# Each PSUM bank of the recurrence and of attention first takes a product of constants

## The chip, the cores and the metric

The kernel runs as one program on one core of a Trainium2 chip. The metric is the time of one launch on the device in microseconds, lower is better. The engines are TensorE (PE in the profile, with its weight loads as PEld), VectorE (DVE), ScalarE (ACT), GpSimd (POOL) and SyncE (SP, which issues most of the transfers). Each engine works through its own list of instructions in order.

## The reference: one inference step of a hybrid decoder layer

512 prompt tokens with 16 learned meta tokens ahead of them, and 8 samples of 4 tokens each, go through one layer with the same weights. All data is float32.

```
h    = rmsnorm(x);  proj = h @ w_in          # 1024 -> 2560 columns: 1792 for the recurrence, 768 for attention
y_rw = rwkv7_time_mix(proj[:, :1792])        # 8 heads x 64; per token S = S*w + (S a) b' + v k',  y = S r
y_at = window_attention(proj[:, 1792:])      # 8 query heads, 2 key heads, the last 128 positions, sinks
x    = x + concat(y_rw, y_at) @ w_out
x    = x + peer(rmsnorm(x))                  # 8 heads choose 16 of 16384 experts each by product keys:
                                             # sum over 128 chosen k of gelu(h . eu[k]) * gate[k] * ev[k]
y    = rmsnorm(x)
```

The outputs are y of prompt and samples, the key and value windows, the state of the recurrence and the last normalised row.

## The kernel before, in words

The prompt is cut into four tiles of 128 tokens, 0 to 3; meta tokens and samples are short pieces of their own. The work falls into a front part (to about 1110 us in the profile) and a dense part.

**Front part.** `project` (L218 and around) multiplies the normalised input by w_in, block of 128 columns by block; the second half of the tokens (`project_rest`, 314 columns a product, PSUM tag pD) stands beside the first pieces of the recurrence. For each tile `rwkv_prep` (L333 to L390, banks pA and pQ) forms the factors of the recurrence, and `wkv_local` (banks pB; pC for the meta tokens) solves a triangular system of 128 steps in blocks: for each of five levels, and for two groups of four heads, a transposition by the identity (L182 on XT), four products of 64 columns into one bank (L492), a copy out by ACT, four products of 64 columns into the next bank (L497), and a masked copy by DVE. `wkv_chain` carries the state across tiles. `attend_prompt`, `attend_sample`, `sample_wkv` and what is around them use banks of the tag pC. `rest` multiplies by w_out (L918) and w_query (L952) into banks of the tag pD, with weights that DMA brings, and picks experts on DVE.

Of the tags pB and pC there are two banks of [128, 512] float32 each. A call of `pB()` or `pC()` hands out the next of the two: whoever writes it first waits until the readers of its last contents are done. 434 banks are handed out in this way in the front part.

**Gathers.** For prompt tile 0, then for the samples and for tile 3, rows of expert tables are fetched one chosen expert at a time (L1032, an indirect DMA that POOL issues, 512 KB into one of five buffers `gat`); DVE forms the dot product or adds the row (L126). They are put in beside the front part, from `first_gathers` on.

**Dense part.** For tiles 1 and 2 all 16384 experts are multiplied (L1401 to L1480).

**What sets the order.** The program is written stage by stage, and a scheduler orders each engine's list by a simulated clock of its own: an instruction is put in when, in that simulation, its inputs and its bank are there. So more work on one engine shifts the order on others. Gathers carry a mark that keeps them behind the front's own work.

Of the kernel before, what the change touches and what calls it, by code (L numbers as in the profile page):

```python
# [46 lines left out]
BF16 = mybir.dt.bfloat16  # L47
# [66 lines left out]
def hymba_step(ctx, tc, x_prompt, x_sample, cache_k, cache_v, state_wkv, state_shift, meta, norm1_g, w_in, mu, w0,  # L114
# [3 lines left out]
    A, G, T, DM = nc.scalar, nc.gpsimd, nc.tensor, nc.sync  # L118
# [14 lines left out]
    def _t(pool, tag, bufs, shape, dt=F32):  # L133
        uid[0] += 1
        return pool.tile(list(shape), dt, tag=tag, name=f"{tag}_{uid[0]}", bufs=bufs)
# [29 lines left out]
    ident = p0.tile([128, 128], F32, name="ident")  # L165
    DM.dma_start(ident, const[:, _OFF["ident"][0]:_OFF["ident"][0] + 128])
    cst = cp.tile([128, _MSO], F32, name="cst")
# [86 lines left out]
    def pA():  # L254
        return _t(pe, "pA", 1, [128, 512])

    def pB():
        return _t(pp, "pB", 2, [128, 512])

    def pC():  # L260
        return _t(pp, "pC", 2, [128, 512])

    def pD():
        return _t(pp, "pD", 2, [128, 512])
# [342 lines left out]
    def wkv_chain(r, l, ycat):  # L607

        ends = r["ends"]
        S0 = st("S0", 1, [128, 4, 64])  # L610
        V.tensor_tensor(S0, Sst, bc(ends[:, :, 1:2], [128, 4, 64]), OP.mult)
        for hb in range(2):
            pb = 64 * hb
            A.copy(Sbd[pb:pb + 64, :, hb, :], S0[pb:pb + 64])
        pC_ = pC()[:, 0:256].rearrange("p (a b) -> p a b", a=4)
        for blk in range(4):
            T.matmul(pC_[:, blk, :], l["M"][:, blk, :], S0[:, blk, :], start=True, stop=True)
        V.tensor_tensor(Sst, pC_, l["Sl"], OP.add)
        V.tensor_tensor(Sst, Sst, bc(ends[:, :, 0:1], [128, 4, 64]), OP.mult)
        pY = pC()  # L620
        for blk in range(4):
            T.matmul(pY[:, 128 * blk:128 * blk + 128], l["R2T"][:, blk, :], Sbd[:, blk].rearrange("p a b -> p (a b)"),
                     start=True, stop=True)
        Y = st("gn", 2, [128, 512])
        V.tensor_tensor(Y, pY, l["Yl"].rearrange("p a b -> p (a b)"), OP.add)
        gn_out(r, Y, ycat)

    def meta_state(r):
        n = r["n"]
        pm = pC()  # L630
        for blk in range(4):
            for hb in range(2):
                h = 2 * blk + hb
                hc = slice(64 * h, 64 * h + 64)
                o = pm[64 * hb:64 * hb + 64, 64 * blk:64 * blk + 64]
                T.matmul(o, r["Bn"][:n, hc], r["RW"][:n, 0, h, :], start=True, stop=False)
                T.matmul(o, r["Kn"][:n, hc], r["Vn"][:n, hc], start=False, stop=True)
        V.tensor_tensor(Sst, pm[:, 0:256].rearrange("p (a b) -> p a b", a=4), bc(r["ends"][:, :, 0:1], [128, 4, 64]),
                        OP.mult)
# [521 lines left out]
    with ExitStack() as px:  # L1161
# [36 lines left out]
        def transposed(h, half, rows):  # L1198
            p = jps().rearrange("p (a b) -> p a b", a=4)
            for j in range(4):  # L1200
                k = 4 * half + j
                transpose(p[:, j, 0:rows], h[:rows, k * 128:(k + 1) * 128])
            return p
# [30 lines left out]
        for half in range(2):  # L1234
            p = transposed(hS, half, 72)
# [45 lines left out]
    pp = fr.enter_context(tc.tile_pool(name="pp", bufs=1, space=PSUM))  # L1281
# [132 lines left out]
    def dps():  # L1414
        return _t(dp, "w", 4, [128, 512])
# [3 lines left out]
    for i in range(2):  # L1419
        hn = dt_("uv", UV, [128, 2, D])[:, 0]  # L1420
        DM.dma_start(hn, hscr[1 + i])
        for half in range(2):
            p = dps().rearrange("p (a b) -> p a b", a=4)
# [168 lines left out]
    for i in range(2):  # L1592
# [3 lines left out]
        for half in range(2):  # L1596
            p = dps()
# [35 lines left out]
```

## Time and profile before

| | us |
|---|---|
| median of 3 runs | 2225.62 |
| lowest, highest | 2205.1, 2230.73 |
| the profiled execution's own time | 2230.96 |
| its span, first to last instruction | 2229.0 |

In the profiled execution TensorE was busy 1852.5 us (83%), VectorE 1712.3 us (77%), GpSimd 1426.3 us (64%) and ScalarE 869.6 us (39%). The mean granted clock of TensorE was 0.869 of full speed. Full speed is 2.4 GHz, and the only other level is half of it, 1.2 GHz; a value between them is a mean over a stretch.

How to read it: the shares are means over stages with different limits, so a stage is looked at by itself. "Busy" of TensorE does not say at which clock it was busy. In the chain of waits "issue" is time in which an engine waited for nothing that the profile shows.

### The profile page before, as it was taken

What the parts mean: (1) busy time and instruction counts of PE and PEld (TensorE: products, weight loads), DVE (VectorE), ACT (ScalarE), POOL (GpSimd) and SP (SyncE); (2) the same over time, 40 slices, a digit from 0 to 9 for tenths busy, and PEclk for the clock granted to TensorE, in tenths of its full rate; (3) what the DMA queues carried; (4) which work ended last, traced back from release to release, by engine and by line L of the source; (5) the groups of instructions that cost most, each with busy time, mean ns of one, the idle gap of its engine ahead of it and who ended that gap; (6) DMA issues with size and microseconds to landing.
All of it is one profiled execution on the core that took longest, in us unless ns stands there. A gap on an engine that the chain in (4) does not pass through costs nothing.

```text
span 2229.0 us, 37454 instructions
## 1 busy us (share of the span) xinstructions
PE 1852.5 (83%) x13915; PEld 1720.4 (77%) x13915; DVE 1712.3 (77%) x3265; ACT 869.6 (39%) x1963; POOL 1426.3 (64%) x1091
## 2 busy tenths in 40 slices
PE   5899975585859858897366898899999999999995
PEld 5889974374737747786366888899999999999995
DVE  5543436788787888799889689987666688999897
ACT  6654421211313324223189534343444444343333
POOL 0110103878674767465615457899898999999996
PEclk9999996555655769998679999999999999999998
DMA  7532472687785798997667887799999999998886
GB/s 219 158 107 75 136 188 86 232 276 236 258 285 161 235 310 292 284 310 236 187 212 253 300 285 250 274 325 335 332 327 330 334 312 322 310 320 307 312 300 210
DMA packets 310156, 569.51 MB, mean 256 GB/s; under 512 B 32787, under 2 KB 194565, under 8 KB 309830
## 3 DMA queue, kind: packets, MB, share of 16 engines
q0 software_dynamic: 84048, 305.70, 39.7%
q1 hardware_dynamic: 225926, 261.43, 36.3%
q8 instruction: 109, 1.79, 0.3%
q14 instruction: 73, 0.60, 0.1%
HBM read 543.07 MB, written 24.60 MB: 255 GB/s over the span
## 4 chain that ended last, share of the span: by engine, by line
PE 38%; DVE 21%; issue 13%; POOL 12%; DMA 11%; ACT 4%; SPq 0%; DVEq 0%; POOLq 0%; ACTq 0%
POOL gat L1032 7%; DVE gat L126 4%; DVE x L126 4%; PE pD L218 3%; PE acc L1479 3%; PE acc L1480 3%; PE w L1463 3%; PE acc L1478 3%; PE w L1460 3%; PE w L1461 3%; DMA gat<-in_expert_u_dram,ei 2%; PE w L1446 2%; POOL aL L1471 2%; POOL vL L1453 2%; DMA gat<-in_expert_v_dram,ei 2%
## 5 line engine op out<-in xcount | busy, mean ns | idle before, releaser
L126 DVE SCALAR_TENSOR_TENSOR x<-gat,act,x 128x1024 f32<-128x1024 f32 x287 | 497.6, 1734 | 27.7 <-DMA gat<-in_expert_v_dram,ei 25.8
L1032 POOL DMA_INDIRECT gat<-in_expert_u_dram,ei x256 | 352.5, 1377 | 111.8 <-DVE pre L126 52.7
L1032 POOL DMA_INDIRECT gat<-in_expert_v_dram,ei x256 | 330.9, 1293 | 141.2 <-DVE x L126 41.3
L1453 POOL TENSOR_TENSOR vL<-uv,vH 128x1024 fp32r<-128x1024 f32 x128 | 314.8, 2460 | 20.7 <-ACT vH L1452 18.6
L1479 PE MATMUL acc<-aL,vH 128*128 128x256 f32 x1024 | 294.6, 289 | 20.1 <-POOL aL L1471 19.8
L1478 PE MATMUL acc<-aH,vH 128*128 128x256 f32 x1024 | 295.0, 296 | 4.0 <-ACT aH L1470 4.0
L1480 PE MATMUL acc<-aH,vL 128*128 128x256 f32 x1024 | 290.4, 285 | 0.0
L1460 PE MATMUL w<-dhH,uH 128*128 128x256 f32 x1024 | 253.7, 285 | 2.8 <-ACT lsc L1549 2.7
L1461 PE MATMUL w<-dhL,uH 128*128 128x256 f32 x1024 | 252.5, 284 | 0.0
L126 DVE CUSTOM_DVE_ANT_0 gat<-gat,h 128x1024 f32<-128x1024 f32 x160 | 213.1, 1341 | 47.3 <-DMA gat<-in_expert_u_dram,ei 45.0
L1452 ACT CAST vH<-uv 128x1024 fp32r<-128x1024 f32 x128 | 134.5, 1051 | 227.3 <-issue 121.9
L1479 PEld LDWEIGHTS acc<-aL,vH 128*128 128x128 f32 x1024 | 198.2, 194 | 26.6 <-POOL aL L1471 26.3
L126 DVE CUSTOM_DVE_ANT_0 gat<-gat,lx 128x1024 f32<-128x1024 f32 x128 | 199.7, 1583 | 8.7 <-DMA gat<-in_expert_u_dram,ei 8.6
L1460 PEld LDWEIGHTS w<-dhH,uH 128*128 128x128 f32 x1024 | 197.4, 193 | 3.5 <-ACT lsc L1549 3.1
L1478 PEld LDWEIGHTS acc<-aH,vH 128*128 128x128 f32 x1024 | 194.8, 194 | 4.5 <-ACT aH L1470 4.5
L1480 PEld LDWEIGHTS acc<-aH,vL 128*128 128x128 f32 x1024 | 198.2, 194 | 0.0
L1461 PEld LDWEIGHTS w<-dhL,uH 128*128 128x128 f32 x1024 | 197.3, 193 | 0.1
L126 DVE TENSOR_TENSOR uL<-w,uH 128x512 fp32r<-128x512 f32 x256 | 167.7, 683 | 11.4 <-ACT uH L1448 9.0
L1463 PE MATMUL w<-dhH,uL 128*128 128x256 f32 x1024 | 154.3, 290 | 12.7 <-DVE uL L126 12.4
L1471 POOL TENSOR_TENSOR aL<-ac,aH 128x256 fp32r<-128x256 f32 x128 | 137.9, 1077 | 29.5 <-ACT aH L1470 27.5
L126 DVE TENSOR_TENSOR ac<-w,gl 128x128 f32<-128x128 f32 x128 | 49.9, 390 | 137.3 <-ACT w L1465 120.1
L1448 ACT CAST uH<-w 128x512 fp32r<-128x512 f32 x256 | 139.5, 590 | 29.7 <-PE w L1446 19.2
(575 smaller groups left out, 4222.0 us busy)
## 6 DMA issues: line engine op xcount, KB each, us to landing
uv<-in_expert_u_dram SPq DMA_DIRECT2D x128, 512.0 KB, 4.6
uv<-in_expert_v_dram SPq DMA_DIRECT2D x128, 512.0 KB, 6.4
wst<-in_w_query_dram SPq DMA_DIRECT2D x48, 512.0 KB, 5.6
wst<-in_w_out_dram SPq DMA_DIRECT2D x24, 512.0 KB, 8.0
wst<-in_w_in_dram SPq DMA_DIRECT2D x20, 512.0 KB, 4.3
h2T<-in_w_in_dram SPq DMA_DIRECT2D x20, 512.0 KB, 4.1
gscr<-uv SPq DMA_DIRECT2D x10, 1024.0 KB, 6.2
gl<-gscr SPq DMA_DIRECT2D x16, 512.0 KB, 5.7
```

The costliest lines, as they stand in the source:

```text
L126: r = getattr(nc.vector, name)(*args, **kw)
L1032: G.indirect_dma_start(out=r, out_offset=None, in_=w[0], in_offset=bass.IndirectOffsetOnAxis(ap=ei[:, k:k + 1], axis=0))
L1448: A.copy(uH[:, ks, :], p)
L1452: A.copy(vH, vn)
L1453: G.tensor_tensor(vL, vn, vH.bitcast(F32), OP.subtract)
L1460: T.matmul(pre, uH[:, k, :], hH[:, k, :], start=(k == 0), stop=False)
L1461: T.matmul(pre, uH[:, k, :], hL[:, k, :], start=False, stop=False)
L1463: T.matmul(pre, uL[:, k, :], hH[:, k, :], start=False, stop=(k == 7))
L1471: return (vH, vL, aH, aL), G.tensor_tensor(aL, ac, aH.bitcast(F32), OP.subtract).ins
L1478: T.matmul(o, vH[:, ds_], aH, start=(j == 0 and d % 2 == 0), stop=False, skip_group_check=True)
L1479: T.matmul(o, vH[:, ds_], aL, start=False, stop=False, skip_group_check=True)
L1480: T.matmul(o, vL[:, ds_], aH, start=False, stop=(j == 127), skip_group_check=True)
```

## The change

`pB()` and `pC()` pass each bank that they hand out through a new helper, which writes all 512 columns of it with one bfloat16 product of constants: the identity's first 128 half-words as weights, 512 half-words of the constants' tile as the moving operand. Nothing reads the result; the real products start with `start=True` and overwrite it. `pA`, `pQ` and `pD` stay as they were.

```diff
+    def in_use(p):
+
+
+        T.matmul(p, ident.bitcast(BF16)[:, 0:128], cst.bitcast(BF16)[:, 0:512], start=True, stop=True)
+        return p
+
     def pB():
-        return _t(pp, "pB", 2, [128, 512])
+        return in_use(_t(pp, "pB", 2, [128, 512]))
 
     def pC():
-        return _t(pp, "pC", 2, [128, 512])
+        return in_use(_t(pp, "pC", 2, [128, 512]))
```

That is 434 more products on TensorE, each with its own weight load: 270 into banks pB and 164 into banks pC. From the insertion on, line numbers are six higher (L497 becomes L503, L333 becomes L339). No other engine has more to do, but the scheduler's order shifts.

TensorE, one level of the recurrence of tile 2, before (XT the matrix that is solved for, XP its transposed copy, LT the triangular factors, ax attention's scores):

```order
L182 MATMUL pB_6280<-ident,XT_6160 128x128 x4
L182 MATMUL pB_6287<-ident,XT_6163 128x128 x4
L492 MATMUL pB_6294<-XP_6285,LT_6088 128x64 x4
L492 MATMUL pB_6300<-XP_6292,LT_6124 128x64 x4
L182 MATMUL pC_4923<-ident,ax_4899 128x128 x4
L497 MATMUL pB_6306<-XT_6160,XP_6285 128x64 x4
L497 MATMUL pB_6312<-XT_6163,XP_6292 128x64 x4
```

The last level of the same tile with the change:

```order
L260 MATMUL pB_6635<-cst,ident 128x512
L182 MATMUL pB_6635<-ident,XT_6453 128x128 x4
L260 LDWEIGHTS ident
L260 MATMUL pB_6643<-cst,ident 128x512
L182 MATMUL pB_6643<-ident,XT_6456 128x128 x4
L260 LDWEIGHTS ident
L260 MATMUL pB_6651<-cst,ident 128x512
L498 MATMUL pB_6651<-XP_6641,LT_6369 128x64 x4
L260 LDWEIGHTS ident
L260 MATMUL pB_6658<-cst,ident 128x512
L498 MATMUL pB_6658<-XP_6649,LT_6411 128x64 x4
L182 MATMUL pC_5182<-ident,ax_5154 128x128 x4
```

Each bank's four products now have the product of constants right ahead of them. So it is for 347 of the 434 banks; for the other 87 some products of other banks stand between, and the last row shows one: bank pC_5182 had its constants twelve rows earlier.

GpSimd, where it forms the factors of tile 2 (pa) between gathers and the samples' outer products (wst), before:

```order
L697 TENSOR_TENSOR wst_4169<-ce_3623,cst 40x512
L697 TENSOR_TENSOR wst_4196<-ce_3623,cst 40x512
L1032 DMA gat_8233<-in_expert_u_dram,ei_9_103 128x1024
L1032 DMA gat_8236<-in_expert_u_dram,ei_9_103 128x1024
L1032 DMA gat_8239<-in_expert_u_dram,ei_9_103 128x1024
L333 TENSOR_TENSOR pa_6023<-m_1243_5987,vecs 128x4x128
```

and with the change:

```order
L1038 DMA gat_8652<-in_expert_u_dram,ei_9_103 128x1024
L703 TENSOR_TENSOR wst_4346<-ce_3743,cst 40x512
L339 TENSOR_TENSOR pa_6304<-m_1243_6268,vecs 128x4x128
L703 TENSOR_TENSOR wst_4376<-ce_3743,cst 40x512
L1038 DMA gat_8655<-in_expert_u_dram,ei_9_103 128x1024
```

Before, 68 gathers stood in GpSimd's list ahead of that row of L333, now 61. The first rows of attention on tile 1 (L740) come behind 163 gathers before and 165 now, and the dense part begins behind 282 in both.

## Rows read from the trace of the kernel before

**Rows 1.** The page: the span in 40 slices, tenths busy, tenths of full clock.

```profile
PE   5899975585859858897366898899999999999995
...
PEclk9999996555655769998679999999999999999998
```

**Rows 2.** Busy time by stretch: stretch, its length, engines, clock, DMA share, GB/s.

```profile
107.00:272.00 165.00, 163.45 (x1326) 143.54 (x1326) 65.35 (x131) 80.27 (x181) 16.55 (x24) 0.98 0.34 97
360.00:573.00 213.00, 139.37 (x920) 111.89 (x920) 167.50 (x300) 43.46 (x102) 153.41 (x108) 0.52 0.66 218
592.00:609.00 17.00, 17.00 (x98) 16.17 (x98) 11.50 (x19) 6.19 (x17) 14.96 (x9) 0.50 0.54 161
633.00:732.00 99.00, 76.17 (x286) 60.89 (x287) 74.74 (x117) 29.18 (x59) 48.80 (x43) 0.50 0.66 214
824.00:920.00 96.00, 81.86 (x563) 72.04 (x562) 72.96 (x133) 32.14 (x86) 59.29 (x53) 0.91 0.94 303
920.00:1110.00 190.00, 134.63 (x1018) 121.73 (x1016) 185.22 (x688) 48.13 (x141) 116.05 (x133) 0.85 0.79 250
```

**Rows 3.** Chain of waits, 205 to 272 us: start, length, what.

```profile
208.01 1.93 PE pB L492 x16
209.94 0.63 PE pD L218 x4
...
211.05 1.93 PE pB L497 x16
212.98 1.64 PE pD L218 x11
...
252.59 6.10 PE pD L218 x42
```

**Rows 4.** Chain of waits, 578 to 732 us: first and last pieces of two stretches.

```profile
592.81 3.31 PE pB L492 x16
596.12 3.41 PE pB L497 x16
...
608.44 0.62 PE pB L550 x3
...
665.61 2.07 PE pB L434 x4
...
716.08 3.71 PE pC L860 x4
...
726.84 3.43 PE pB L497 x16
```

**Rows 5.** Chain of waits, 518 to 545 us: its shares, and one piece.

```profile
by line: issue 37.4%; DVE gat L126 19.0%; DMA gat<-in_expert_u_dram,ei 18.9%; POOL pa L333 9.0%; DVE kt L126 6.8%; POOL gat L1032 6.6%; POOL pa L336 3.9%; DVE XT L126 2.4%; DVE AK L126 2.2%; DVE pa L126 1.3%; DVE pre L126 0.5%; POOLq L1032 
...
523.59 2.44 POOL pa L333
```

**Rows 6.** Gathers alone by stretch: GpSimd's time and their count, clock, DMA.

```profile
400.00:560.00 160.00, 106.46 (x69) 0.52 0.73 244
...
633.00:732.00 99.00, 39.17 (x36) 0.50 0.66 214
732.00:824.00 92.00, 55.24 (x48) 0.65 0.81 275
```

**Rows 7.** Busy time by stretch, as in rows 2, for the clock.

```profile
205.00:235.00 30.00, 30.00 (x340) 27.94 (x339) 7.80 (x14) 12.88 (x36) 0.00 (x0) 1.00 0.31 92
...
706.00:731.00 25.00, 25.00 (x102) 20.57 (x102) 11.34 (x17) 3.71 (x9) 6.46 (x6) 0.50 0.45 142
```

**Rows 8.** Chain of waits, 824 to 920 us: its shares.

```profile
by line: DMA wst<-in_w_query_dram 17.6%; issue 11.0%; DVE x L126 10.1%; PE pD L952 9.4%; PE pD L918 6.1%; POOL gat L1032 4.4%; PE pB L443 4.3%; DVE ax L126 2.5%; PE pB L433 2.2%; PE pD L182 2.0%; DVE XT L126 1.9%; PE pB L182 1.8%; POOL rope
```

**Rows 9.** TensorE's waits, 360 to 830 us: total, times, longest.

```profile
PE pB L443 <- DVE AK L126: 25.6, 5, 12.5
PE pB L184 <- DVE XT L126: 23.3, 4, 12.5
```

## The prediction, written before the changed kernel had run

> **What bounds the kernel now.** I began with the page's slices, which show where TensorE is busy and at which clock [rows 1]: the clock digit drops to 5 to 7 in slices 7 to 15, which are part of the front, and is 9 almost everywhere in the dense part. The change adds work to the front alone, and ahead of the dense part the same 282 gathers stand as before, so I carry the dense part over unchanged and look at the front by stretch [rows 2]. Three kinds of stretch come out.
>
> From 107 to 272 us TensorE is busy 163.45 of 165 us at clock 0.98 [rows 2], and the chain of waits there alternates between wide projection products (pD) and the narrow products of tile 0's recurrence (pB) [rows 3]: TensorE is the bound, at full clock.
>
> From 360 to 573 us the clock is 0.52 and TensorE is busy 139.37 of 213 us [rows 2], but the end is not set by it. Where tile 2's factors are formed, the chain is issue time, gathers, their DMAs and DVE [rows 5]: the gathers and GpSimd's list are the bound.
>
> In 592 to 609 and most of 633 to 732 us the chain is on TensorE at clock 0.50 [rows 2, 4]. The chain's pieces from 665.61 to 726.84 us are 34 of TensorE's with 59.9 us in all, the rest of the 64.7 us being ScalarE and issue; from 592.81 to 608.44 us there are nine pieces with 16.2 us. Together 76.1 us of the chain are TensorE at half clock. From 920 to 1110 us VectorE is busy 185.22 of 190 us [rows 2]: there it is the bound, and products of constants cost nothing; if VectorE's cover were gone, the 57 banks first used there would cost 57 x 0.237 = 13.5 us.
>
> **The price of one added product.** No row has a 512-column product of one pass. The nearest is the projection's run of 42 products of 314 columns in 6.10 us, 0.145 us each [rows 3]; by columns that is 0.145 x 512 / 314 = 0.237 us at full clock and 0.474 at half. From above: L860, which has 512 float32 columns, takes 3.71 / 4 = 0.93 us a record at half clock [rows 4]. From below: zero, where TensorE would have waited. I take 0.237 and 0.474, since the run of wide products is nearest in kind. The page "TensorE: Matmul & The Clock Gate" of the Trainium skill (section "Back-to-back issue gap") has N / 2.4 + 2.5 ns for an isolated product at full clock, 0.216 us here; by it the first term below would be 25.7 us and not 28.2.
>
> **Term 1, the saturated stretch.** By TensorE's new order, 119 of the 434 products stand ahead of the last product of the projection, that is in 107 to 272 us. TensorE has 1.55 us of idle time there to hide them in. 119 x 0.237 = +28.2 us. Behind it stands the first w_out product, whose weights need buffers that the projection holds, so the delay passes on.
>
> **Term 2, the half-clock stretches.** 52 banks have their first product there (13 and 39, counted by laying the order over the trace). What the added products do depends on the clock. That a full clock is to be had with these narrow products is shown by 205 to 235 us: the same L492 and L497 with wide pD products between them, TensorE busy 30.00 of 30 us, clock 1.00; while in 706 to 731 us, busy 25.00 of 25 us with few wide products between, it is 0.50 [rows 7]. What the engine does, not that it is busy, goes with the clock; and the change puts a wide product ahead of every narrow group. At full clock 16 records of L492 take 1.93 us and not 3.31, those of L497 1.93 and not 3.41 [rows 3, 4], so the price falls by 42.5%: at most 76.1 x 0.425 = 32.4 us. If a share q of that time comes to full clock, the term is -32.4 q + 52 x (0.237 q + 0.474 (1 - q)) = 24.6 - 44.7 q. Its bounds are +24.6 (q = 0) and -20.1 (q = 1). I take q = 0.8, or -11.2: the five levels of a tile are transpositions and 64-column products, nearest to 205 to 235 us once wide products stand between; the entry from 665 us (L434 and the like, on 64 rows) I count as staying at half. The gathers allow it: 36 of them stand in 633 to 732 us, and at the 92 / 48 = 1.9 us each of the next stretch they need 69 of its 99 us [rows 6].
>
> **Term 3, 824 to 920 us.** The clock is 0.91 already [rows 2], so there is little to win. The listed TensorE pieces of the chain come to 9.4 + 6.1 + 4.3 + 2.2 + 2.0 + 1.8 = 25.8% [rows 8], with the unlisted small ones perhaps 40%. 38 banks x 0.237 x 0.4 = +3.6 us; bounds 0 and 9.0.
>
> **Term 4, GpSimd's order.** Seven gathers fewer, 61 in place of 68, stand ahead of L333 of tile 2, which is on the chain [rows 5]. A gather there takes 160 / 69 = 2.3 us [rows 6], so tile 2 can start 16 us sooner; but attention on tile 1 now has 165 gathers ahead of it in place of 163, so they must be made good in between. Between 0 and -16 I take -5, nearer to nothing, since they stand in the same list. The other banks (82 in 360 to 573 us, 50 in 730 to 824, and the few that are left) lie beside the gathers' chain: zero; their cover is the gathers, and without it the 82 alone would cost 82 x 0.474 = 39 us.
>
> **Sum.** 28.2 - 11.2 + 3.6 - 5 = +15.6 us. On the profiled execution's 2230.96 us (span 2229.0 and 1.96 around it) that is 2246.6. That execution lies 5.3 us above the median of the runs, 2225.62, so as a median I expect **2241 us**. With the terms' bounds but q between 0.5 and 1 the forecast's own range is about 2215 to 2258. What a measurement here can tell from no change is about 1%, 22 us: below 2203 is faster, above 2248 slower. Chance of this case: 0.45.
>
> **Rival 1, the clock stays at half (slower; 0.22).** Place: the stretches of term 2. Price: q = 0, so 28.2 + 24.6 + 3.6 - 5 = +51 us, about 2277. It decides if one wide product for each four narrow ones is too few. For it speaks that in 706 to 731 us wide pieces such as L860 are there and do not lift the clock [rows 4, 7]. Against it speaks 205 to 235 us, though with more wide products than the change brings. The Trainium skill's page "TensorE: Matmul & The Clock Gate" (section "Why this matters for your kernels") asks for TensorE to be kept busy without gaps for the full clock; by that rule more work in a stretch that is busy throughout changes nothing, which is this rival's result. The trace does not agree that being busy suffices, as 706 to 731 us shows.
>
> **Rival 2, a product of constants that waits (slower; 0.13).** 87 of the 434 stand apart from their bank's own products, put where the simulated clock says that the bank is free. Where DVE or ACT empties it later on the chip, all of TensorE's list waits behind it. TensorE's waits for DVE in 360 to 830 us were up to 12.5 us [rows 9]. Two such waits more on the chain make about 2241 + 20 = 2261 us. Against it: in much of that stretch the chain passes beside TensorE.
>
> **Rival 3, everything pays (faster; 0.20).** q = 1 and term 4 in full give 28.2 - 20.1 + 3.6 - 16 = -4 us. If the clock rises in 360 to 573 us as well, TensorE's 139.37 us shrink by up to 0.425, or 59 us; the chain hardly passes there, but if a quarter shows, through tiles that get ready sooner, that is -15: together -19, about 2206. Against it: the chain [rows 5], and long stretches without any product in which nothing can lift the clock.
>
> **Range and chances.** 2200 to 2285 takes in the forecast's bounds, Rival 1's 2277 with some spread, and most of Rival 3. Slower by over 1%: all but a little of Rival 1 (0.20), more than half of Rival 2 (0.08) and a quarter of the forecast (0.12), 0.40. Faster: two thirds of Rival 3 with a trace of the forecast, 0.14. Within 1%: 0.46.
>
> **What would show it.** In the changed profile: the end of the projection near 300 us and not 272, with TensorE busy throughout (term 1); the mean price of L260 near 0.24 us at full clock; tile 2's levels at a clock above 0.8, with 16 records of L498 near 2 us (term 2; 0.50 there is Rival 1); among TensorE's waits new rows of L260 for DVE or ACT (Rival 2); a stretch from 360 us at clock well above 0.52, and shorter (Rival 3). I am wrong altogether if the dense part differs in length, or if the front's end does not move with term 1.

## The result, and the profile after

The changed kernel takes 2258.78 us (median of 4 runs, 2255.87 to 2264.25) where the kernel before took 2227.64 us on the same chip: ratio 1.0140, 95% interval [1.0104, 1.0175], 31 us slower. The profiled execution took 2264.25 us with a span of 2262.1 us, 33.1 us more than before, and its mean granted clock rose from 0.869 to 0.892. The forecast was 2241 us, range 2200 to 2285: sign and range hold, the size does not.

The page of the changed kernel, the slices that answer to [rows 1]:

```profile
PE   5999979697868858997646897899999999999995
...
PEclk9999989556775959997878999999999999999998
```

In slices 10 to 14 the clock digits are 6, 7, 7, 5, 9, where they were 5, 6, 5, 5, 7. Stretches of the changed kernel, columns as in [rows 2]:

```profile
107.00:312.00 205.00, 197.79 (x1468) 161.56 (x1471) 67.71 (x142) 80.26 (x181) 17.88 (x26) 0.97 0.29 83
400.00:600.00 200.00, 159.40 (x864) 106.07 (x869) 150.89 (x258) 43.22 (x102) 142.33 (x99) 0.57 0.67 222
760.00:785.00 25.00, 23.93 (x196) 19.09 (x198) 20.05 (x25) 11.09 (x28) 20.00 (x15) 0.93 0.86 288
```

The stretch that was 107 to 272 us is now 107 to 310 us. The end of tile 2's levels, 760 to 785 us, is at 0.93; the gathers' stretch from 400 us stays near half, at 0.57. Two stretches of 30 and 25 us as in [rows 7], the second in tile 2's levels:

```profile
205.00:235.00 30.00, 29.75 (x289) 24.02 (x289) 5.54 (x12) 10.59 (x29) 0.00 (x0) 1.00 0.16 47
740.00:765.00 25.00, 22.39 (x149) 17.95 (x149) 21.52 (x27) 7.34 (x16) 17.04 (x15) 0.94 0.85 292
```

The levels that were busy 25.00 of 25 us at 0.50 are now busy 22.39 of 25 us at 0.94.

The chain of waits of the changed kernel from 107 to 312 us (its shares, then its last long pieces), which answers to [rows 3]:

```profile
by line: PE pD L218 27.7%; DMA h2T<-in_w_in_dram 8.2%; PE pB L260 6.5%; PE pC L260 6.4%; PE pB L498 4.2%; PE pB L503 4.1%; PE pB L182 2.6%; DMA wst<-in_w_out_dram 2.2%; PE pB L439 2.1%; PE pC L184 2.1%; ACT wst L213 2.0%; PE pQ L184 2.0%; P
...
261.17 5.86 PE pD L218 x40
...
273.50 5.59 DMA h2T<-in_w_in_dram
...
288.30 6.07 DMA h2T<-in_w_in_dram
...
296.78 5.12 DMA h2T<-in_w_in_dram
...
304.34 4.90 PE pD L218 x22
```

L260 is the product of constants: 6.5 + 6.4% of 205 us is 26.4 us. New in the chain is its end: from 272 us on the projection waits for its weights (h2T), block after block. The last product ends at 309.4 us, 41 us later than before.

The instructions of L260 over the whole span (durations in ns: least, median, most), and what ended TensorE's idle time ahead of them:

```profile
L260 PEld LDWEIGHTS <-ident x434: 95/100/291, 102.9 to 1112.0; 128*128 128x128 bf16 x145
L260 PE MATMUL pB<-cst,ident x258: 376/389/634, 103.3 to 1029.9; 128*128 128x512 bf16 x129
L260 PE MATMUL pC<-cst,ident x158: 376/389/634, 102.9 to 1111.5; 128*128 128x512 bf16 x158
...
  DVE RB L126: 30.2, 8
  issue: 27.0, 65
  DVE XT L126: 8.6, 8
```

TensorE's waits from 390 to 860 us (total, times, longest), for [rows 9]:

```profile
PE pB L260 <- DVE RB L126: 14.2, 4, 6.1
...
PE pB L449 <- DVE AK L126: 11.3, 4, 4.1
...
PE pB L260 <- DVE XT L126: 8.1, 7, 2.4
```

The new waits of L260 have taken the place of the real products' waits; none is longer than the 12.5 us of before. The dense part begins 28.2 us later than before (1144.3 us, and 1116.1):

```profile
L1432 PE MATMUL w<-ident,uv x16: 273/421/444, 1144.3 to 1147.6; 128*128 128x128 f32 x16
```

So 41 us were lost up to the projection's end and 13 us came back behind it. From the dense part's begin to the span's end it is 1117.8 us against 1112.9.

### The profile page after: what moved, and what is told of

Its sections match the earlier page's. It is cut to its first block, busy times and chain, and to the rows that moved or that the text cites. A ratio compares the mean times of both kernels' runs of the same rounds, so it can differ in the third digit from the quotient of the medians.

```text
span 2262.1 us, 38234 instructions
## 1 busy us (share of the span) xinstructions
PE 1933.7 (85%) x14331; PEld 1733.8 (77%) x14349; DVE 1693.3 (75%) x3265; ACT 872.7 (39%) x1964; POOL 1446.4 (64%) x1091
## 4 chain that ended last, share of the span: by engine, by line
PE 41%; DVE 23%; POOL 11%; issue 11%; DMA 10%; ACT 4%; SPq 0%; DVEq 0%; POOLq 0%; ACTq 0%
POOL gat L1038 6%; DVE gat L126 5%; DVE x L126 4%; PE acc L1485 3%; PE acc L1486 3%; PE acc L1484 3%; PE w L1469 3%; PE w L1466 3%; PE w L1467 3%; PE pD L218 3%; DMA gat<-in_expert_v_dram,ei 2%; PE w L1452 2%; POOL aL L1477 2%; PE pD L958 2%; PE ps L218 2%
## 5 line engine op out<-in xcount | busy, mean ns | idle before, releaser
L126 DVE SCALAR_TENSOR_TENSOR x<-gat,act,x 128x1024 f32<-128x1024 f32 x287 | 487.7, 1699 | 36.0 <-DMA gat<-in_expert_v_dram,ei 34.5
L1038 POOL DMA_INDIRECT gat<-in_expert_u_dram,ei x256 | 349.4, 1365 | 111.7 <-DVE pre L126 48.1
L1038 POOL DMA_INDIRECT gat<-in_expert_v_dram,ei x256 | 346.6, 1354 | 115.3 <-issue 33.6
L126 DVE CUSTOM_DVE_ANT_0 gat<-gat,h 128x1024 f32<-128x1024 f32 x160 | 203.1, 1280 | 49.3 <-DMA gat<-in_expert_u_dram,ei 43.2
L126 DVE CUSTOM_DVE_ANT_0 gat<-gat,lx 128x1024 f32<-128x1024 f32 x128 | 204.6, 1622 | 3.4 <-DMA gat<-in_expert_u_dram,ei 3.4
L126 DVE TENSOR_TENSOR uL<-w,uH 128x512 fp32r<-128x512 f32 x256 | 167.5, 682 | 11.9 <-ACT uH L1454 9.4
L126 DVE TENSOR_TENSOR ac<-w,gl 128x128 f32<-128x128 f32 x128 | 49.9, 389 | 147.4 <-ACT w L1471 132.1
L1454 ACT CAST uH<-w 128x512 fp32r<-128x512 f32 x256 | 139.4, 590 | 27.8 <-PE w L1452 17.4
```

The source lines that it names most:

```text
L126: r = getattr(nc.vector, name)(*args, **kw)
L1038: G.indirect_dma_start(out=r, out_offset=None, in_=w[0], in_offset=bass.IndirectOffsetOnAxis(ap=ei[:, k:k + 1], axis=0))
L1454: A.copy(uH[:, ks, :], p)
```

## Experiments

**First theory** (the prediction's): the products cost 0.24 us each in the saturated stretch, and the higher clock pays some of it back behind. **Rival:** the products hardly matter, and the scheduler's shifted lists, or a limit of the projection itself, make the time. Each ratio is to the kernel before, run on the same chip beside it.

**Products from the first `rest` on alone** (324 banks, behind the projection):

```diff
+    warm = [False]
     def in_use(p):
+        if not warm[0]:
+            return p
         T.matmul(p, ident.bitcast(BF16)[:, 0:128], cst.bitcast(BF16)[:, 0:512], start=True, stop=True)
...
     project_rest()
+    warm[0] = True
```

> The product of constants is left out for the 110 banks handed out up to the end of the projection and of tile 0's recurrence, and kept for the 324 behind. Theory A (the loss is made in the saturated stretch from 107 us on, and the later stretches give some of it back through a higher clock): 10 to 15 us faster than before, about 2214 us, with the projection ending near 268 us as before and tile 2's levels at a clock well above 0.50. Theory B (the later stretches give nothing; the 13 us that come back behind the projection are slack in which the delay was absorbed): no delay, so nothing to absorb, and only the price of the products is left: 2228 to 2245 us. Theory C (the scheduler's shift of gathers is the gain): like A, but with tile 2's levels still at half clock.

Measured: 2219.54 us, ratio 0.9973 [0.9947, 0.9999]; projection's end at 269.6 us, dense part at 1108.4 us. **Products up to there alone** (110 banks; the flag the other way round):

> The reverse: the product of constants only for the 110 banks up to the end of the projection and of tile 0's recurrence. Theory A: the projection ends near 309 us, 41 us later than before, and nothing gives it back: about 2266 us, slower than the change itself (2259). Theory B: slack absorbs 13 of the 41 us here too: about 2256 us, as the change or a little faster.

Measured: 2270.15 us, ratio 1.0201 [1.0150, 1.0252]; projection's end at 304.6 us. Both speak for the first theory: the early banks lose the time. Without them the kernel is 0.27% faster, 6 us where that theory gave 10 to 15, with tile 2's levels at a clock of 0.88. The early banks alone come out 0.6% slower than all 434, with intervals that overlap; if that is real, the later banks give something back, through the clock or through the lists.

**All 434 products with 128 columns.** `p[:, 0:128]` and `cst[:, 0:128]` in place of 512:

> All 434 products of constants, but of 128 columns in place of 512. If the price goes by columns (0.06 us each), the projection ends 7 to 15 us later than before and not 41, the clock of tile 2's levels falls back towards 0.50, and the total is 2228 to 2242 us. If what costs is a product's weight load, its wait for the bank or the scheduler's order, the projection still ends at 295 us or later, and the total is about 2250 us.

Measured: 2233.72 us, ratio 1.0036 [1.0003, 1.0069]; projection's end at 280.8 us, 12.9 later than before. In tile 2's levels (here and below from the second level's first L492 to L558) the clock is back near the 0.66 of before:

```profile
700.00:759.00 59.00, 55.70 (x357) 47.79 (x356) 45.24 (x53) 17.92 (x45) 39.22 (x34) 0.69 0.74 250
```

The price by columns that the expectation named fits the projection's end and the total. And yet in this execution the dense part begins at 1112.4 us, 3.7 us sooner than before: 16.6 us come back behind the projection with almost no rise of the clock, which the first theory does not explain. How much of that is the kernel's own is not sure: the execution is one of its fastest (2229.27 us), and over all runs it is 0.36%, 8 us, slower than before, so that only about 5 of the 12.9 us come back.

**The change, and a second buffer for the loads of the projection's last blocks:**

```diff
-            wt = st("h2T", 1, [128, 8, 128])
+            wt = dx([128, 8, 128]) if blk > 12 and blk % 2 else st("h2T", 1, [128, 8, 128])
```

> The change, and every second of the projection's last blocks loads its weights into another buffer, so that a load need not wait for the splitting of the block ahead. Theory A1 (about 14 of the 41 us are the last five blocks, which go by load, split, multiply one after the other at 7.3 us each, since fewer of them fit beside the recurrence): the projection ends near 296 us and not 309, and the total is 8 to 13 us below the change, about 2248 us. Theory A2 (all 41 us are TensorE's own time for 119 products, 0.34 us each): no difference, 2259 us.

Measured: 2246.88 us, ratio 1.0105 [1.0070, 1.0140]; its projection ends at 294.4 us, 15 us sooner than the change's (the group's first and last start):

```profile
L218 PE MATMUL pD<-gat,wst x360: 301/308/498, 114.0 to 294.1; 128*128 128x314 f32 x180
```

The last blocks now start 4.3 us apart (272.6, 277.0, 281.3, 285.6, 289.9) and not 7 to 8 (272.8, 280.2, 287.2, 295.5, 303.1). The load of one block after another through one buffer is what the projection's tail waits for. In the total about 8 of the 15 us are left (1.0105 and 1.0140, with intervals that overlap), as the first of the two theories had it.

**The lists held, the columns changed.** The four kernels so far change the lists of all engines with every edit. So I let the scheduler order the 324-bank kernel, and only then set the columns of the products in the finished lists: lists made for 512 columns and products of 16; lists made for 16 columns and products of 512; and both 16. In the edit `names` are the products of constants.

```diff
     with tile.TileContext(nc, schedule_with_timeline_sim=True) as tc:
+        CONST.clear()
         hymba_step(tc, *args)
...
+                if i.name in names:
+                    o, x = i.outs[0], i.ins[0]
+                    b.instructions[k] = i.__replace__(outs=[o.__replace__(ap=[o.ap[0], (1, 16)])],
+                                                      ins=[x.__replace__(ap=[x.ap[0], (1, 16)]), i.ins[1]])
...
```

> The kernel with the products from rest(0) on alone (324 banks), every engine's list of instructions exactly as there, but each product of constants writes 16 columns in place of 512. Two theories of what the products give back behind the projection. Theory clock: the wide products raise the granted clock in the levels of tiles 1 and 2; at 16 columns tile 2's levels fall back from 0.88 to near 0.67 and take 55 us or more in place of 52, and the total comes to 2225 to 2234. Theory order: the shifted order of the lists gives the time back; the total stays at 2212 to 2221 though the clock falls.

> The mirror of it: every engine's list as the scheduler makes it for products of 16 columns in the same 324 banks, but each writes 512 columns when it runs. Theory clock: tile 2's levels at a clock above 0.8, total 2212 to 2223. Theory order: the clock rises as well, but the wide products only cost, total 2228 to 2240.

> Products of 16 columns in the same 324 banks, the lists made for them. Theory clock: clock of tile 2's levels near 0.67 and total 2226 to 2234, that is, no gain. Theory order says only that it differs from the kernel with the same lists and wide products by no more than the wide products' own cost, so 2222 to 2235 where that one has 2228 to 2240.

| 324 banks | products of 16 columns | products of 512 columns |
|---|---|---|
| lists made for 512 | 0.9989 [0.9958, 1.0020] | 0.9973 [0.9947, 0.9999] |
| lists made for 16 | 1.0110 [1.0068, 1.0151] | 1.0095 [1.0063, 1.0126] |

Along a row, where nothing but the columns differs, the ratio falls by 0.15%, less than the intervals can tell from nothing. (The 0.9973 is from another chip than the other three, each with the kernel before beside it.) Down a column it moves by 1.2%, 27 us. The stretch from tile 1's state product (L558) to tile 2's shows that the clock did rise; lists for 512, products of 16 and then of 512:

```profile
601.00:758.00 157.00, 129.05 (x666) 106.21 (x665) 120.08 (x183) 43.37 (x100) 102.76 (x85) 0.57 0.72 238
```

```profile
605.00:752.00 147.00, 119.14 (x661) 87.44 (x661) 118.60 (x181) 43.22 (x100) 102.11 (x84) 0.73 0.76 253
```

From 0.57 to 0.73, and 10 us shorter: the clock's gain is there, and most of it is spent elsewhere, since the ratios differ by 0.16%, less than 4 us. Lists for 512 with 16 columns came out as the theory of the clock had it: tile 2's levels take 63 us at a clock of 0.58, and 2232.56 us lies in its range. But the kernel before took 2232.59 us beside it, so that against it no loss is shown. With lists for 16, 2249.10 and 2255.60 us lie beyond what either theory gave: neither had the lists' own 27 us.

**324 banks and the second load buffer:**

> The products from rest(0) on alone, and every second of the projection's last seven blocks loads its weights into a buffer of its own. If the blocks behind tile 0's recurrence are bound by that one buffer before the change too, the projection ends 3 to 8 us sooner than at 269.6 us and the total is 2209 to 2217; if TensorE alone is the bound there, nothing moves: 2217 to 2222.

Measured: 2238.12 us, ratio 1.0055 [1.0023, 1.0087], projection's end at 283.2 us, 14 us later than without the buffer. Both expectations fell: the edit moved the lists again, and seven whole blocks of the projection now stand behind tile 0's L558 where four did. So the second buffer is shown to help only where the tail is long.

**The lists of before, products put in.** Here the scheduler orders the kernel before; then a product of constants is put into TensorE's list right ahead of the first product of each bank, with that product's waits. All other engines' lists are those of before.

```diff
     with tile.TileContext(nc, schedule_with_timeline_sim=True) as tc:
         hymba_step(tc, *args)
...
+            if o.memref[:3] in ("pB_", "pC_") and o.memref not in seen:
+                seen.add(o.memref)
...
+                    out.append(i.__replace__(
+                        name=nc.get_next_instruction_name(), outs=[o.__replace__(ap=[(512, 128), (1, 512)], offset=0)],
...
+                        sync_info=mybir.SyncInfo(on_wait=list(i.sync_info.on_wait) if i.sync_info else [], on_update=[])))
+        out.append(i)
...
```

> The kernel before with every engine's list as it was, and the 434 products of 512 columns put into TensorE's list after the ordering, each right ahead of the first real product of its bank (and with that product's waits). Theory products: the change is slower by what the products take in 107 to 272 us: the projection ends 26 us later, near 294 us or beyond, little comes back behind it, total 2250 to 2260, ratio 1.009 to 1.014. Theory lists: the changed order of the lists is what costs; with the old lists the projection still ends later, but the total is at 0.997 to 1.006 of the kernel before.

> The same with the last 324 of the 434 banks alone, all behind the projection. If the higher clock pays more than the products take: ratio 0.990 to 0.997, tile 2's levels at a clock above 0.8 and shorter than 56.2 us. If price and gain are even, as the pairs with equal lists and 16 or 512 columns say (0.15% apart): 0.997 to 1.001. If products with no gain: 1.002 or more.

Measured: all 434, 2270.85 us, ratio 1.0192 [1.0161, 1.0223]; the last 324, 2245.81 us, ratio 1.0084 [1.0058, 1.0111]. The products cost without any shift of the lists, more than either theory gave, and 0.5% more than in the changed kernel (intervals that overlap a little). Behind the projection they do not pay on the old lists.

Then the other two corners: **the changed lists with 16 columns**, and **the old lists with 16 columns**.

> The changed kernel, every engine's list as there, with products of 16 columns in place of 512. Theory products: the projection ends near 275 to 283 us and not 309, total 2226 to 2240, ratio 0.998 to 1.005. Theory lists: the order of the lists costs by itself, so ratio 1.008 to 1.016 with the projection still beyond 290 us.

> The kernel before with every engine's list as it was and all 434 products put into TensorE's list, of 16 columns each. Theory lists: small products cost nearly nothing, so the 30 us that the projection ends late under the changed lists with 16 columns are the lists' own; here the projection ends at 268 to 276 us and the ratio is 0.998 to 1.004. Rival: a product with its weight load costs much even at 16 columns; the projection ends at 285 us or later and the ratio is 1.008 or more, and then the lists cost less than 10 us.

Measured: changed lists, 16 columns: 2257.98 us, ratio 1.0139 [1.0108, 1.0170]; old lists, 16 columns: 2256.82 us, 1.0134 [1.0081, 1.0186]. The changed lists came out as the theory of the lists had it, with the projection's end at 298.1 us; the old lists as the rival of that expectation had it, with 288.7 us. First and last start of the projection's largest group in old lists with 16 columns, old lists with 512, and changed lists with 16:

```profile
L218 PE MATMUL pD<-gat,wst x360: 301/308/630, 118.1 to 288.4; 128*128 128x314 f32 x180
```

```profile
L218 PE MATMUL pD<-gat,wst x360: 301/308/630, 118.4 to 297.1; 128*128 128x314 f32 x180
```

```profile
L219 PE MATMUL pD<-gat,wst x360: 301/308/629, 116.3 to 297.8; 128*128 128x314 f32 x180
```

But the rival's reason, that a small product is dear, is only half of it: with 16 columns the clock fell too. TensorE from 160 to 195 us, before and then on the old lists with 16 columns (with 512 the clock is 1.00 there):

```profile
160.00:195.00 35.00, 35.00 (x270) 31.02 (x270) 12.17 (x26) 16.01 (x38) 1.41 (x1) 1.00 0.27 80
```

```profile
160.00:195.00 35.00, 35.00 (x203) 30.30 (x202) 8.61 (x19) 12.47 (x31) 1.41 (x1) 0.76 0.20 59
```

A product's own price is read where the clock is full in all three kernels: from the projection's 195th product to its 358th, with 54 products of constants between; before, old lists with 16 columns, and with 512:

```profile
181.80:234.50 52.70, 52.70 (x521) 49.02 (x520) 16.42 (x33) 21.62 (x53) 0.00 (x0) 1.00 0.31 92
```

```profile
195.00:252.30 57.30, 57.30 (x575) 53.02 (x574) 16.24 (x33) 21.54 (x53) 0.00 (x0) 1.00 0.29 85
```

```profile
193.50:259.80 66.30, 64.52 (x564) 54.84 (x574) 16.47 (x33) 22.16 (x53) 0.00 (x0) 1.00 0.25 74
```

That is 4.6 us more for 54 products of 16 columns, 0.085 us each, and 13.6 us more with 512, 0.25 us each. Over all stretches that can be laid side by side in this way, 88 products, it is 0.089 and 0.256 us.

All of it together, from the profiled executions (us from the span's start):

| | before | old lists, 16 | old lists, 512 | changed lists, 16 | the change |
|---|---|---|---|---|---|
| projection's end | 268.0 | 288.7 | 297.4 | 298.1 | 309.4 |
| of its 20 blocks, behind tile 0's L558 | 4 | 4 | 4 | 8 | 8 |
| first w_query's end | 352.2 | 371.8 | 381.6 | 375.3 | 389.3 |
| tile 1's L558 | 611.1 | 630.8 | 647.9 | 616.4 | 634.0 |
| tile 2's L558 | 764.2 | 791.4 | 792.4 | 776.9 | 783.8 |
| tile 3's L558 | 983.2 | 1010.7 | 1017.7 | 1018.2 | 1022.0 |
| dense part's begin | 1116.1 | 1146.2 | 1148.5 | 1139.0 | 1144.3 |
| ratio | 1 | 1.0134 | 1.0192 | 1.0139 | 1.0140 |

Each column of times is one execution, and the runs of one of these kernels spread by 8 to 31 us; so differences of a few us, in the late rows above all, are not sure. The ratios rest on all runs.

Four readings follow. At the projection's end both parts add up: small products cost 20.7 us on the old lists, the other 496 columns 8.7 us (old lists) or 11.3 us (changed), and the changed lists 9.4 us (16 columns) or 12.0 us (512). Of the 20.7 us about 10 are the products (110 x 0.089) and about 11, an estimate by what is left, go with the clock, which from 107 us to the projection's end is 0.91 with 16 columns, 0.98 before and 0.97 with 512. Of the 29.4 us with 512 columns 28 are the products (110 x 0.256). The lists' part goes with the eight blocks, not four, that they put behind tile 0's recurrence, where the one load buffer binds. Behind the first w_query the changed lists give back: at the dense part's begin they are 7.2 us (16) and 4.2 us (512) better than the old ones. The ratios have 0.05% worse and 0.52% better (12 us) for the same two pairs, so the size of what they give back in the end is open. And from tile 1's L558 to tile 2's the columns alone are worth 160.6 - 144.5 = 16.1 us on the old lists and 160.5 - 149.8 = 10.7 us on the changed ones. There, changed lists with 16 columns and the change:

```profile
616.00:777.00 161.00, 136.13 (x669) 111.99 (x670) 120.45 (x185) 43.54 (x100) 104.67 (x86) 0.53 0.72 240
```

```profile
634.00:784.00 150.00, 120.27 (x666) 87.19 (x671) 120.73 (x184) 43.77 (x100) 107.98 (x86) 0.73 0.76 249
```

TensorE's busy time falls by 16 us with 496 columns more in each product, since the clock goes from 0.53 to 0.73. The same stretch before, then on the old lists with 16 and with 512 columns:

```profile
611.00:764.00 153.00, 120.27 (x585) 98.11 (x585) 118.56 (x173) 45.45 (x100) 90.35 (x83) 0.60 0.70 228
```

```profile
631.00:791.00 160.00, 134.23 (x663) 111.41 (x665) 116.52 (x171) 45.53 (x100) 90.19 (x85) 0.55 0.68 222
```

```profile
648.00:792.00 144.00, 108.97 (x656) 83.78 (x667) 116.08 (x172) 45.69 (x100) 98.98 (x85) 0.79 0.73 242
```

One limit of this cut: a product that was put in waits for the inputs of the real one too, so it cannot run ahead in a wait as 87 of the change's can. The old lists' price behind the projection is so an upper one; in the saturated stretch, where TensorE hardly waits (busy 187.04 of 190.4 us with 512 columns), this weighs little.

## Why the prediction was right or wrong

**Term 1 (+28.2 us forecast, +41.4 measured) is the step that was mis-sized.** The products' part of it holds: put into the old lists they cost 297.4 - 268.0 = 29.4 us, and the chain of the changed kernel has 26.4 us of them. What the term did not have is the 12.0 us of the lists. I counted the products that stand ahead of the last wide one and did not look at where the wide ones went, though the order had it before any run: eight blocks behind tile 0's recurrence in place of four. "TensorE busy throughout" failed with it, since the tail waits for loads.

That 28.2 and 29.4 are so close is partly luck. On the old lists 110 products stand ahead of the last wide one, not 119 (nine more come ahead only because the wide ones moved back), and one costs 29.4 / 110 = 0.267 us on the mean, 0.25 to 0.26 where the clock is full in both, and not 0.237. And I took the price in proportion to columns (0.145 x 512 / 314), which would give 0.007 us at 16 columns, where a product costs 0.085 to 0.089. One place where it can be seen at full clock, TensorE on the old lists, with 16 and then with 512 columns:

```profile
197.46 0.19 PE L492 MATMUL pB<-cst,ident 128*128 128x16 bf16 x1
197.50 1.08 PE L492 MATMUL pB<-XP,LT 128*128 128x64 f32 x8
198.43 0.17 PE L492 MATMUL pB<-cst,ident 128*128 128x16 bf16 x1
```

```profile
196.13 0.39 PE L492 MATMUL pB<-cst,ident 128*128 128x512 bf16 x1
196.36 1.00 PE L492 MATMUL pB<-XP,LT 128*128 128x64 f32 x8
197.20 0.38 PE L492 MATMUL pB<-cst,ident 128*128 128x512 bf16 x1
```

A bank with its product takes 0.97 us with 16 columns and 1.07 with 512: the narrow one lets the next group start after 0.04 us and not 0.23, but that group then takes 0.93 us and not 0.84. The records show a weight load of 0.10 us for each product, near the whole price of the narrow one; that it is the cause is not shown. From start to start the wide product's 0.23 us is near the 0.216 us that the Trainium skill gives for an isolated one ("TensorE: Matmul & The Clock Gate", "Back-to-back issue gap"). The same page's section "LDWEIGHTS (loading the stationary operand)" gives columns / 1.2 ns, 107 ns for these weights; the traces come near it, with medians of 100 and 104 ns in the change and in the changed lists with 16 columns.

**Term 2 (-11.2 us, q = 0.8): mechanism right in tile 2, and nothing came of it in tile 1.** The clock of tile 2's levels went from 0.66 to 0.94, as forecast; before and with the change:

```profile
708.00:764.00 56.00, 51.17 (x287) 43.97 (x288) 36.10 (x43) 17.05 (x42) 27.44 (x28) 0.66 0.63 205
```

```profile
732.00:784.00 52.00, 48.24 (x357) 39.41 (x360) 43.58 (x56) 20.42 (x47) 39.85 (x30) 0.94 0.80 265
```

The stretch that ends with these levels is 8.6 us shorter than before on the old lists with 512 columns, and 3.3 us in the changed kernel, whose lists differ. The levels shrank from 56.2 to 48.3 us on the old lists and to 51.4 us in the changed kernel. On the old lists with 16 and with 512 columns:

```profile
727.30:791.50 64.20, 64.20 (x335) 56.35 (x333) 36.24 (x43) 17.25 (x42) 27.94 (x30) 0.52 0.62 203
```

```profile
744.00:792.00 48.00, 42.00 (x328) 34.33 (x332) 37.79 (x44) 17.11 (x42) 32.22 (x31) 1.00 0.78 255
```

At twice the clock they are 16 us shorter, which is all of the 16.1 us above; TensorE, which filled them at half clock, no longer does. The stretch ahead of them takes 96 to 97 us before, with 16 columns and with 512, at clocks of 0.56, 0.58 and 0.68: it is not shorter, as I had counted the entry. Tile 1's levels take 47.0 us at 0.70 before and 52.1 us at 0.88 with the change: there the chain is no longer led by TensorE but by gathers and DVE (POOL gat L1038 17.4%, issue 17.3%, DVE gat L126 13.3%; L498, its largest line, 8.3%), and the part of the term that I put there did not come.

**The banks priced at zero** cost something. On the old lists the stretch from the first w_query's end to tile 1's L558 grew by 7.4 us; in the four pairs with held lists, 512 columns in place of 16 cost 3.5 to 7.3 us there, though the gathers bound it. **Term 3** (+3.6 us, bounds 0 to 9) measured +6.3 us on the old lists from tile 2's L558 to tile 3's.

So the products come to 29.4 + 7.4 - 8.6 + 6.3 - 2.1 (the last stage) = +32.4 us at the dense part's begin, where terms 1 to 3 had +20.6. What they cost behind the projection is an upper figure, by the limit above.

**Term 4 (-5 us, 0 to -16)** stood for the lists. They are worth -4.2 us, the change against the old lists with the same products: +12.0 at the projection's end, which the term did not have, and -16.2 behind. With 16 columns, where a product that waits weighs less, the lists give -16.6 us behind the projection, so the limit of the cut changes little here; the ratios have -0.5% in place of -4.2 us, about -12 us. What the term named is there: tile 2's L333 starts 160.3 us behind the first w_query's end and not 171.4, and tile 1's L558 244.7 us behind it and not 258.8. And so is what it feared, that passed gathers must be made good: from tile 2's L558 to tile 3's it is 19.2 us longer, then 10.6 us shorter to the dense part. 32.4 - 4.2 = 28.2 us; with the 4.9 us by which the rest of the span is longer, that is the 33.1 us of the spans. I forecast no difference for that rest. It was 1114.2 to 1117.8 us in the profiles of the change and of all twelve kernels of the experiments, and 1112.9 in that of before; why is open.

That the forecast's -12.6 us behind the projection (terms 2 to 4) and the measured -13.2 us agree is luck: the products are worth +3.0 us there in place of -7.6, and the lists -16.2 in place of -5. One sum of the forecast was off, too: the bounds of its terms, with q between 0.5 and 1, give 2218 to 2265 us and not 2215 to 2258.

**Rival 1** (clock stays at half) is out: 0.94. **Rival 2** (a product that waits) did not come: the longest wait of L260 in that stretch is 6.1 us, in place of the real product's. **Rival 3** was right in one thing, that the front without the saturated stretch would not lose: 324 banks alone came out at 0.9973. That the clock made this so is not shown: the same products on the old lists cost 0.84%, and on their own lists the columns are worth 0.15% between intervals that overlap.

What stays open is why the scheduler's lists for one set of banks differ by 1.2% between a 16- and a 512-column product. The 324-bank kernel is the fastest seen, by an interval that nearly touches 1, and I would not credit the products for it.

## What to carry to other kernels

Where a scheduler orders the lists, an edit changes two things. Separate them before explaining either: hold the lists and change the instruction, or hold the instruction and change the lists. Work added to a saturated stretch was lost there in full, and it also moved what stood beside it, so look in the new order for where the displaced pieces land and which buffer feeds them. A raised clock shortened a stretch only where TensorE led its chain, and products that buy it must cost less than they win: here 10 to 16 us were won in one stage, and no pair with equal lists shows a gain in the total beyond its intervals. Before a small product is called dear, look at the clock: half of what the small ones cost here was the clock that fell.

## What the hardware showed that I had not expected

A product of 16 columns among float32 groups costs 0.085 to 0.089 us in a saturated stretch at full clock and one of 512 columns 0.25 to 0.26 us: 32 times the columns, three times the price. Small products did not lift the clock, and it fell with them, though TensorE was busy throughout: on the same lists the clock from 160 to 195 us was 1.00 before and 0.76 with products of 16 columns, busy 35.00 of 35 us both times. From tile 1's L558 to tile 2's it was 0.60 before, 0.55 with 434 products of 16 columns on the same lists, and 0.79 with 512 columns, busy 120, 134 and 109 us. These are single executions; on the changed lists the clock from 107 us to the projection's end was 0.94 with 16 columns and 0.97 with 512.
